# Feed-forward second projection: the last part as plain products by token blocks, sums on GpSimd, other places for the operands

## The chip, the cores and the metric

One Trainium2 chip, one core. The time is the device time of one execution in microseconds; of several executions the median is given. Matmuls run on TensorE (PE), the other work on VectorE (DVE), ScalarE (ACT) and GpSimd (POOL); SyncE (SP) issues transfers. Each of these engines takes its instructions in the order in which they stand in its own queue. Projections and their sums use PSUM banks of 128x512 float32; everything else lies in SBUF or in DRAM.

## What is computed

One encoder layer, windowed attention and a SwiGLU feed-forward network, on a sequence of 2048 tokens with D = 1024 and a hidden width of 2816, all in float32:

```
def swiglu(h, w_in, w_out):
    a, b = jnp.split(h @ w_in, 2, axis=-1)
    return (jax.nn.silu(a) * b) @ w_out

        x = x + g1 * rmsnorm(y, mix_norm_post[i])
        h = rmsnorm(x, ffn_norm_pre[i]) * (1.0 + sc2) + sh2
        y = swiglu(h, ffn_w_in[i], ffn_w_out[i])
        x = x + g2 * rmsnorm(y, ffn_norm_post[i])
```

The change concerns `swiglu` and the last line alone.

## The kernel before

A float32 operand is split into a part `hi`, rounded to fp32r, and the rest `lo` (`split`, L152 a cast on ACT, L153 a subtraction on DVE), and a product is three matmuls: hi·hi, hi·lo, lo·hi. On top of that both projections use Strassen-Winograd's scheme: of a 2x2 block product with operands a11, a12, a21, a22 (weights) and b11, b12, b21, b22 (activations), seven products of sums and differences are made where plain multiplication makes eight. For it the weights need s1 to s4, the activations t1 to t4, and the results seven sums.

**First projection.** The sequence is worked in two halves of 1024 tokens. A half has 22 hidden blocks `Hidden` (seven steps, pc0 to pc6, of 12 matmuls each, L147 to L149, into 6 PSUM banks); the last two blocks of a half are interleaved with the loading of the next half's operands (`interleaved`). ACT copies the first step's bank out (`take`, p1, L823); the other steps are added up by DVE. Two blocks make a pair of gated activations b11, b12, b21, b22, and `give_pair` stores its seven operands b11, t3, b22, t1, b21, t2, t4 in DRAM (g_d): for parts in `SPLIT` already split (a cast gh on ACT, a subtraction gl on DVE, two transfers, L799 and L800), else whole (one transfer). Between the stores the differences are formed in place on POOL and DVE.

**Second projection.** For each half the 11 pairs are taken in four parts of 2 or 3 pairs (`PARTS`, (hf, p) names a part, m its pairs). A part has seven stages, one for each product; a stage has four token blocks of 128, and a block m x 3 matmuls into one of 6 banks po (L1031 to L1033). In a half's first part ACT copies the banks to 28 result tiles z (L1036), later parts add to them on DVE (L1038). In a half's last part, as soon as the results of a block are complete, `SUMS` adds seven of them up (L1042), four on DVE and three on POOL per block. `Weights` loads raw weights wr (1 MB each, L976), forms s1, s3, s2, s4 on POOL (L979, L980, L998, L1000) and splits them into 14 buffers wo; `Grams` loads the stored activations into 15 buffers g (L1018, with a split on arrival, or L1020, both halves at once). Both run four stages ahead of the products. `finish(hf, b)` ends a token block: loads of x, squares and their sum on ACT (L1062), the root by Ln and Exp (L1067, L1068), eight small operations of DVE, transposes px of x on PE (L1079), then on DVE the scaled result (L1080) and the sum with x (L1081), and the store of out (L1082). The first half's endings are dealt out between the products of part (1,0); those of the second half follow the last products.

**What sets the order.** The program is recorded and a scheduler puts the instructions of each engine in order by the readiness of their operands and by the place where they are written; a stretch marked `high_priority(offset=...)` is taken as if it were written earlier. Tiles of one tag are reused in a ring, so a load or a split waits for the last reader of the tile it replaces.

## Time and profile before

| | us |
|---|---|
| median of 3 executions | 2247.26 (2245.46 to 2250.28) |
| the profiled execution's own time | 2245.18 |
| its span, first to last instruction | 2243.4 |
| PE busy | 2062.5 (92% of the span) |
| DVE busy | 1645.6 (73%) |
| POOL busy | 1154.7 (51%) |
| ACT busy | 1077.6 (48%) |
| mean granted TensorE clock | 0.959 |
| second projection, first matmul | 1752.0 |
| last matmul of the second projection | 2216.84 |

Busy time counts instructions that run, not what they wait for. A row of a timeline gives the start, the duration, the engine and line, the output and the inputs, the count of alike instructions in a run, and in brackets how long the engine had stood idle before it and what released it. A row of a stretch gives its length and then, for PE, weight loads, DVE, ACT and POOL, the busy time and the number of instructions. A group's row gives busy time, mean duration in ns, and the idle time in front with what ended it.

### The profile page before, as it was taken

What the parts mean: (1) busy time and instruction counts of PE and PEld (TensorE: products, weight loads), DVE (VectorE), ACT (ScalarE), POOL (GpSimd) and SP (SyncE); (2) the same over time, 40 slices, a digit from 0 to 9 for tenths busy, and PEclk for the clock granted to TensorE, in tenths of its full rate; (3) what the DMA queues carried; (4) which work ended last, traced back from release to release, by engine and by line L of the source; (5) the groups of instructions that cost most, each with busy time, mean ns of one, the idle gap of its engine ahead of it and who ended that gap; (6) DMA issues with size and microseconds to landing.
All of it is one profiled execution on the core that took longest, in us unless ns stands there. A gap on an engine that the chain in (4) does not pass through costs nothing.

```text
span 2243.4 us, 28903 instructions
## 1 busy us (share of the span) xinstructions
PE 2062.5 (92%) x9351; PEld 1674.8 (75%) x9351; DVE 1645.6 (73%) x2554; ACT 1077.6 (48%) x2135; POOL 1154.7 (51%) x1018
## 2 busy tenths in 40 slices
PE   5897999999988887999999879999999399999996
PEld 4785788878777665778887768888888288878885
DVE  7667665576768378876778898878785769695669
ACT  4536566686778545343434544444342554243222
POOL 3305444465986666866676655555552513353322
PEclk8997999999999998999999989999999699999998
DMA  7898867566564753545445854434342744659653
GB/s 260 238 273 286 260 162 219 148 204 183 174 200 149 220 174 122 177 138 171 163 158 185 285 187 162 148 137 165 129 170 76 264 145 154 241 207 366 247 204 131
DMA packets 287139, 431.01 MB, mean 192 GB/s; under 512 B 86739, under 2 KB 153868, under 8 KB 284940
## 3 DMA queue, kind: packets, MB, share of 16 engines
q1 hardware_dynamic: 286988, 429.16, 57.9%
q8 instruction: 74, 1.21, 0.2%
q14 instruction: 77, 0.63, 0.1%
HBM read 291.16 MB, written 137.92 MB: 191 GB/s over the span
## 4 chain that ended last, share of the span: by engine, by line
PE 32%; DVE 8%; POOL 4%; issue 4%; DMA 3%; ACT 2%; SPq 0%; POOLq 0%; DVEq 0%; ACTq 0%
PE pc_i L147 6%; PE pc_i L148 6%; PE pc_i L149 6%; PE po L1031 4%; PE po L1033 4%; PE po L1032 4%; DVE z L1042 1%; DMA wr<-w_out 1%; DVE z L1038 1%; DVE z L1080 1%; DVE wo_s L153 1%; DVE wo_a L153 1%; DMA ly<-y_d 1%; DVE wa_i L153 1%; POOL ws L979 0%
## 5 line engine op out<-in xcount | busy, mean ns | idle before, releaser
L147 PE MATMUL pc_i<-ht,ws_i 128*128 128x512 f32 x528 | 208.6, 396 | 6.7 <-ACT p_i L823 6.7
L148 PE MATMUL pc_i<-ht,ws_i 128*128 128x512 f32 x528 | 207.4, 393 | 0.9 <-DVE ht L153 0.9
L149 PE MATMUL pc_i<-ht,ws_i 128*128 128x512 f32 x528 | 207.4, 393 | 0.0
L456 DVE CUSTOM_DVE_ANT_0 pr<-s,bias,nsink 128x288 f32<-128x288 f32 (+3 forms) x256 | 123.5, 497 | 66.8 <-PE s L453 55.4
L458 ACT ACTIVATE pr<-pr,nm 128x289 f32<-128x289 f32 (+3 forms) x256 | 135.2, 530 | 74.0 <-DVE nm L456 65.2
L462 POOL TENSOR_SCALAR pr<-pr,rs 128x288 f32<-128x288 f32 (+3 forms) x256 | 138.7, 562 | 61.8 <-DVE rs L460 61.7
L153 DVE TENSOR_TENSOR wa_i<-wiri,wa_i 128x512 fp32r<-128x512 f32 x132 | 148.9, 1128 | 21.4 <-ACT wa_i L152 21.4
L1038 DVE TENSOR_TENSOR z<-po,z 128x512 f32<-128x512 f32 x168 | 113.5, 684 | 51.6 <-PE po L1033 50.1
L153 DVE TENSOR_TENSOR ws_i<-s_i,ws_i 128x512 fp32r<-128x512 f32 x132 | 136.6, 1035 | 19.4 <-ACT ws_i L152 19.2
L1031 PE MATMUL po<-wo_s,g 128*128 128x512 f32 x352 | 137.5, 394 | 11.6 <-ACT wo_s L152 11.0
L148 PE MATMUL pc_i<-hb,wa_i 128*128 128x512 f32 x352 | 139.1, 395 | 3.7 <-DVE hb L153 3.7
L1032 PE MATMUL po<-wo_s,g 128*128 128x512 f32 x352 | 138.2, 393 | 4.0 <-DVE wo_s L153 4.0
L149 PE MATMUL pc_i<-hb,wa_i 128*128 128x512 f32 x352 | 139.1, 395 | 1.8 <-DVE wa_i L153 1.8
L147 PE MATMUL pc_i<-hb,wa_i 128*128 128x512 f32 x352 | 139.7, 397 | 0.0
L1033 PE MATMUL po<-wo_s,g 128*128 128x512 f32 x352 | 138.0, 392 | 0.0
L475 PE MATMUL t<-ident,pr 128*128 128x128 f32 x736 | 118.6, 283 | 17.5 <-DVE plo L153 7.0
L979 POOL TENSOR_TENSOR ws<-wr 128x512 f32<-128x512 f32 x22 | 32.2, 1464 | 195.4 <-DMA wr<-w_out 195.4
L153 DVE TENSOR_TENSOR plo<-t,phi 128x512 fp32r<-128x512 f32 x184 | 121.9, 681 | 14.7 <-ACT phi L152 13.6
L152 ACT CAST wa_i<-wiri 128x512 fp32r<-128x512 f32 x132 | 81.5, 618 | 106.1 <-PE pc_i L149 103.1
L852 POOL TENSOR_TENSOR p_i<-p_i,u_i 128x512 f32<-128x512 f32 x44 | 67.0, 1523 | 126.0 <-issue 64.9
L453 PE MATMUL s<-k,q 128*128 128x288 f32 (+4 forms) x512 | 115.8, 326 | 15.7 <-DVE nm L456 15.3
L152 ACT CAST ws_i<-s_i 128x512 fp32r<-128x512 f32 x132 | 81.5, 618 | 93.6 <-PE pc_i L149 88.7
(281 smaller groups left out, 6391.4 us busy)
## 6 DMA issues: line engine op xcount, KB each, us to landing
wiri<-w_in SPq DMA_DIRECT2D x88, 512.0 KB, 4.6
g<-g_d_t SPq DMA_DIRECT2D x56, 512.0 KB, 5.4
ada<-ada_w SPq DMA_DIRECT2D x48, 512.0 KB, 5.7
wr<-w_out SPq DMA_DIRECT2D x22, 1024.0 KB, 8.9
g<-g_d_b SPq DMA_DIRECT2D x42, 512.0 KB, 4.9
q_d<-eq SPq DMA_DIRECT2D x64, 256.0 KB, 4.9
q<-q_d SPq DMA_DIRECT2D x16, 1024.0 KB, 6.8
wor<-w_o SPq DMA_DIRECT2D x32, 512.0 KB, 4.5
```

The costliest lines, as they stand in the source:

```text
L147: pe.matmul(ps, w[0], h[0], start=first, stop=False)
L148: pe.matmul(ps, w[0], h[1], start=False, stop=False)
L149: pe.matmul(ps, w[1], h[0], start=False, stop=last)
L152: act.copy(hi, src)
L153: return eng.tensor_tensor(lo, src, f(hi), ALU.subtract).ins
L456: dve.tensor_tensor_reduce(pr[:, i, lo:hi], ps[:, :n], bias[g][:, lo - starts[i]:hi - starts[i]], -1.0, nsink[:, g:g + 1], ALU.add, ALU.mi ...
L458: act.activation(pr[:, i, lo:hi + 1], pr[:, i, lo:hi + 1], AF.Exp, bias=nm[:, i:i + 1], scale=-1.0, accum_out=rs[:, i:i + 1])
L462: pool.tensor_scalar(pr[:, i, lo:hi], pr[:, i, lo:hi], rs[:, i:i + 1], 1.0, ALU.mult, ALU.mult)
L1031: pe.matmul(ps, g[:, 0], w[:, 0], start=k == 0, stop=False)
L1032: pe.matmul(ps, g[:, 0], w[:, 1], start=False, stop=False)
L1033: pe.matmul(ps, g[:, 1], w[:, 0], start=False, stop=k == m - 1)
L1038: dve.tensor_tensor(z[hf, b, name], ps, z[hf, b, name], ALU.add)
```

## The change

Five edits that belong together:

- The last part (1,3), pairs 9 and 10 of the second half, is no longer made by Strassen-Winograd but as plain products, `plain(j, b)`: eight times 24 matmuls, straight into the results' places. Its pairs are stored as b11, b12, b21, b22 without differences, and its weights are used as they are.
- The sums are all on POOL, seven for a block. The first half's stay in part (0,3); the second half's move from (1,3) to (1,2).
- `finish` takes one row block of 128 tokens (j, b) and multiplies by the gain row before the root is known; the second half's endings follow block by block behind `plain`.
- Part (0,3), pairs 8 to 10 of the first half, is stored whole and split when it is loaded.
- The pools rp (raw weights), gp (activations) and wo (weights) are opened on one side and in this order; wo has 11 buffers, gp 12, and three stages ahead are put at the start, the weights written ahead of the activations.

```diff
-SPLIT = ((0, 3), (1, 0), (1, 1), (1, 2), (1, 3))
+LAST = (1, 3)
+SPLIT = ((1, 0), (1, 1), (1, 2), (1, 3))
...
+        if (hf, part_of[hf][j][0]) == LAST:
+            for n in b:
+                give(n, b[n], False)
+            return
...
+    PLAIN = (("a11", "b11"), ("a12", "b21"), ("a21", "b12"), ("a22", "b22"))
-    SUMS = {"1": (("2", "1", pool),), "6": (("6", "1", dve), ("1", "6", "5", pool)),
-            "7": (("7", "6", dve), ("4", "7", pool), ("5", "7", dve)), "3": (("3", "1", dve),)}
+    SUMS = {"1": (("2", "1"),), "6": (("6", "1"), ("1", "6", "5")), "7": (("7", "6"), ("4", "7"), ("5", "7")),
+            "3": (("3", "1"),)}
-    WB, GB, G0 = 14, 15, 5
-
+    WB, GB = 11, 12
+
+    rp = open_pool(ctx, "rp")
+    gp = open_pool(ctx, "gp")
     wo = open_pool(ctx, "wo")
-    gp = open_pool(ctx, "gp")
-    rp = open_pool(ctx, "rp", side="right")
...
+                if (hf, p) == LAST:
+                    self.src.append(dict(a11=a11, a12=a12, a21=a21, a22=a22))
+                    continue
...
-        if p == len(PARTS[hf]) - 1:
-            for x, *y, eng in SUMS.get(name, ()):
+        if (hf, p) in ((0, len(PARTS[0]) - 1), (1, len(PARTS[1]) - 2)):
+            for x, *y in SUMS.get(name, ()):
                 y = [x] + y if len(y) == 1 else y
-                eng.tensor_tensor(z[hf, b, x], z[hf, b, y[0]], z[hf, b, y[1]], ALU.add)
+                pool.tensor_tensor(z[hf, b, x], z[hf, b, y[0]], z[hf, b, y[1]], ALU.add)
...
+    def plain(j, b):
+
+        hf, p = LAST
+        for i in range(2):
+            ps = psO.tile([P, CH], F32, tag="p", name=f"pl{j}_{b}_{i}")
+            m = PARTS[hf][p]
+            for k in range(m):
+                for e in range(2):
+                    g = [grams.g[hf, p, x, k] for x in range(4) if PLAIN[x][1] == f"b{e + 1}{j + 1}"][0][:, :, b * P:(b + 1) * P]
+                    w = [wts.w[hf, p, x, k] for x in range(4) if PLAIN[x][0] == f"a{i + 1}{e + 1}"][0]
+                    pe.matmul(ps, g[:, 0], w[:, 0], start=k == e == 0, stop=False)
+                    pe.matmul(ps, g[:, 0], w[:, 1], start=False, stop=False)
+                    pe.matmul(ps, g[:, 1], w[:, 0], start=False, stop=k == m - 1 and e == 1)
+            y = z[hf, b, PLACE[i, j]]
+            dve.tensor_tensor(y, ps, y, ALU.add)
+
+    def finish(hf, j, b):
+
+        c = hf * CPH + j
+        x1 = yp.tile([P, KT, P], F32, tag="x1", name=f"x1_{c}_{b}", bufs=3)
+        sp.dma_start(x1, x1_d[c][:, :, b * P:(b + 1) * P])
         yield
...
+        for i in range(2):
+            sq = yp.tile([P, CH], F32, tag="sq", name=f"sq{c}_{b}_{i}", bufs=2)
+            act.activation(sq, ys[i], AF.Square, scale=D ** -0.5, accum_out=ss[:, i:i + 1])
+            dve.tensor_tensor(ys[i], ys[i], grow[:, i * CH:(i + 1) * CH], ALU.mult)
+            px.append(psF.tile([P, CH], F32, tag="mm", name=f"px{c}_{b}_{i}"))
+            for k in range(JB):
+                pe.transpose(px[i][:, k * P:(k + 1) * P], x1[:, i * JB + k, :], ident)
+        dve.scalar_tensor_tensor(v, ss[:, :1], EPS, ss[:, 1:], ALU.add, ALU.add)
         act.activation(r, v, AF.Ln)
         act.activation(r, r, AF.Exp, scale=-0.5)
...
+        for i in range(2):
+            dve.scalar_tensor_tensor(ys[i], ys[i], r, px[i], ALU.mult, ALU.add)
+            (act if hf and i else sp).dma_start(out[c, b, :, i * CH:(i + 1) * CH], ys[i])
+        yield
...
     with tc.high_priority(offset=400):
-        grams.load(4)
-        wts.put(4)
+        wts.put(3)
+        grams.load(3)
...
+    last = [finish(LAST[0], j, b) for j in range(CPH) for b in range(JB)]
+    next(last[0])
+    for n, (j, b) in enumerate((j, b) for j in range(CPH) for b in range(JB)):
+        plain(j, b)
+        for f_ in last[n + 1:n + 2]:
+            next(f_)
+        for _ in last[n]:
+            pass
```

Line numbers behind the change differ: the casts and subtractions of `split` are L153 and L154, the copy p1 L828, the copies z L1048, the additions z L1050, the sums L1054, the weights' operations L991, L992, L1010 and L1012.

ACT, at the change of halves in the first projection: before (gh0_10 is the splitting of the first half's last pair for its store, hb and ht the next half's operands, ws, wa weights, p1_i1_0 the copy of the next half's first bank).

```order
L152 CAST ws2_i1_2_12907<-s2_i1_2_12898 128x512
L152 CAST gh0_10_t3_12526<-u2_i0_20_12267 128x512
L152 CAST gh0_10_b22_12531<-u2_i0_21_12282 128x512
L152 CAST wa12_i1_2_12910<-wiri1_2_12894 128x512
L152 CAST ws3_i1_2_12913<-wiri1_2_12894 128x512
L152 CAST gh0_10_t1_12538<-p1_i0_20_12221 128x512
L152 CAST gh0_10_b21_12543<-p1_i0_21_12236 128x512
L152 CAST ws1_i1_2_12916<-s1_i1_2_12897 128x512
L152 CAST gh0_10_t2_12550<-u2_i0_21_12282 128x512
L152 CAST wa22_i1_2_12919<-wiri1_2_12894 128x512
L152 CAST gh0_10_t4_12555<-p1_i0_21_12236 128x512
L823 COPY p1_i1_0_12620<-pc0_i1_0_12607 128x512
```

The same place on ACT after the change:

```order
L153 CAST ht41_3_12442<-ht41_3_12442 128x512
L153 CAST ws4_i1_0_12533<-s4_i1_0_12510 128x512
L153 CAST ws4_i1_1_12671<-s4_i1_1_12648 128x512
L853 ACTIVATE u2_i0_20_12227<-u2_i0_20_12227 128x512
L853 ACTIVATE u2_i0_21_12242<-u2_i0_21_12242 128x512
L153 CAST hb221_0_12489<-hb221_0_12489 128x512
L828 COPY p1_i1_0_12549<-pc0_i1_0_12536 128x512
L153 CAST wa11_i1_2_12833<-wiri1_2_12823 128x512
L153 CAST hb221_1_12493<-hb221_1_12493 128x512
L153 CAST hb221_2_12497<-hb221_2_12497 128x512
```

The casts gh0_10 are gone, and the copy p1_i1_0 stands directly behind the first of the last four operand casts.

ACT, at the start of the second projection, before: the first copies of results, z0_0_5 and on, and what stands ahead of them (wo0_1 and g0_1 are the weights and activations of the second part, (0,1)).

```order
L152 CAST g0_1_0_1_16392<-g0_1_0_1_16392 128x512
L152 CAST wo0_1_s1_0_16376<-ws0_1_0_16363 128x512
L152 CAST g0_1_0_2_16396<-g0_1_0_2_16396 128x512
L152 CAST wo0_1_s1_1_16380<-ws0_1_1_16368 128x512
L1050 COPY growt_16171<-pgrow_16169 8x128
L1036 COPY z0_0_5_16182<-po0_0_0_0_16175 128x512
L1036 COPY z0_1_5_16191<-po0_0_0_1_16184 128x512
L1036 COPY z0_2_5_16200<-po0_0_0_2_16193 128x512
L1036 COPY z0_3_5_16209<-po0_0_0_3_16202 128x512
L1036 COPY z0_0_2_16232<-po0_0_1_0_16225 128x512
```

The same place after the change (g0_0_4 to g0_0_6 are the activations of the first part's last stages):

```order
L153 CAST g0_0_4_1_16142<-g0_0_4_1_16142 128x512
L153 CAST g0_0_5_0_16188<-g0_0_5_0_16188 128x512
L153 CAST g0_0_5_1_16192<-g0_0_5_1_16192 128x512
L153 CAST g0_0_6_0_16238<-g0_0_6_0_16238 128x512
L153 CAST g0_0_6_1_16242<-g0_0_6_1_16242 128x512
L1062 COPY growt_16042<-pgrow_16040 8x128
L1048 COPY z0_0_5_16053<-po0_0_0_0_16046 128x512
L1048 COPY z0_1_5_16062<-po0_0_0_1_16055 128x512
L1048 COPY z0_2_5_16071<-po0_0_0_2_16064 128x512
L1048 COPY z0_3_5_16080<-po0_0_0_3_16073 128x512
L1048 COPY z0_0_2_16103<-po0_0_1_0_16096 128x512
```

The copies stood behind casts of part (0,1), weights included; now they stand behind casts of activations of part (0,0), and the weights of (0,1) come later.

POOL, at the end of the first half's sums, before (z0_b_n are results, ws1_0 and wr1_0 weights of part (1,0), ws1_1 and wr1_1 of part (1,1)):

```order
L980 TENSOR_TENSOR wr1_0_2_17745<-wr1_0_2_17745 128x512
L998 TENSOR_TENSOR ws1_0_2_17747<-ws1_0_2_17747,wr1_0_2_17745 128x512
L1042 TENSOR_TENSOR z0_0_4_16407<-z0_0_4_16407,z0_0_7_16467 128x512
L1000 TENSOR_TENSOR wr1_0_2_17745<-wr1_0_2_17745,ws1_0_2_17747 128x512
L1042 TENSOR_TENSOR z0_1_4_16416<-z0_1_4_16416,z0_1_7_16476 128x512
L1042 TENSOR_TENSOR z0_2_4_16425<-z0_2_4_16425,z0_2_7_16485 128x512
L1042 TENSOR_TENSOR z0_3_4_16434<-z0_3_4_16434,z0_3_7_16494 128x512
L979 TENSOR_TENSOR ws1_1_0_18427<-wr1_1_0_18425 128x512
L980 TENSOR_TENSOR wr1_1_0_18425<-wr1_1_0_18425 128x512
```

The same place after the change:

```order
L1054 TENSOR_TENSOR z0_1_4_16262<-z0_1_4_16262,z0_1_7_16337 128x512
L1054 TENSOR_TENSOR z0_1_5_16062<-z0_1_5_16062,z0_1_7_16337 128x512
L1054 TENSOR_TENSOR z0_0_3_16388<-z0_0_3_16388,z0_0_1_16153 128x512
L1054 TENSOR_TENSOR z0_1_3_16397<-z0_1_3_16397,z0_1_1_16162 128x512
L1054 TENSOR_TENSOR z0_2_4_16271<-z0_2_4_16271,z0_2_7_16346 128x512
L1054 TENSOR_TENSOR z0_2_5_16071<-z0_2_5_16071,z0_2_7_16346 128x512
L1054 TENSOR_TENSOR z0_2_3_16406<-z0_2_3_16406,z0_2_1_16171 128x512
L1012 TENSOR_TENSOR wr1_0_2_17716<-wr1_0_2_17716,ws1_0_2_17718 128x512
L1054 TENSOR_TENSOR z0_3_3_16415<-z0_3_3_16415,z0_3_1_16180 128x512
L1054 TENSOR_TENSOR z0_3_4_16280<-z0_3_4_16280,z0_3_7_16355 128x512
L1054 TENSOR_TENSOR z0_3_5_16080<-z0_3_5_16080,z0_3_7_16355 128x512
L991 TENSOR_TENSOR ws1_1_0_18398<-wr1_1_0_18396 128x512
```

Between the last weights of (1,0) and the first of (1,1) the queue now holds the sums into z0_b_3 and z0_b_5 too, which DVE made before.

More of the change, by code (lines that the diff above doesn't have):

```diff
@@ L93, in encoder_layer @@
     part_of = [[(p, k) for p, m in enumerate(PARTS[i]) for k in range(m)] for i in range(S // HALF)]
-    g_d = [[{n: dram.tile([P, 2 if (i, part_of[i][j][0]) in SPLIT else 1, CH], F32, name=f"g_d{i}_{j}_{n}") for n in OPERANDS}
+    g_d = [[{n: dram.tile([P, 2 if (i, part_of[i][j][0]) in SPLIT else 1, CH], F32, name=f"g_d{i}_{j}_{n}") for n in OPERANDS + ("b12",)}
             for j in range(HT // 2)] for i in range(S // HALF)]
@@ L962, in encoder_layer, with names @@
     parts = [(hf, p) for hf in range(S // HALF) for p in range(len(PARTS[hf]))]
-    stages = [(part, i) for part in parts for i in range(len(PRODUCTS))]
+    stages = [(part, i) for part in parts for i in range(len(PLAIN if part == LAST else PRODUCTS))]
+    def names(part, i):
+        return (PLAIN if part == LAST else PRODUCTS)[i][:2]
     class Weights:
@@ L990, in put @@
                     self.load(hf, p)
-                name = PRODUCTS[i][0]
+                name = names((hf, p), i)[0]
                 for k, src in enumerate(self.src):
@@ L998, in put @@
                         pool.tensor_tensor(src["s2"], src["s1"], src["a11"], ALU.subtract)
-                    elif name == "a12":
+                    elif name == "a12" and (hf, p) != LAST:
                         pool.tensor_tensor(src["s4"], src["a12"], src["s2"], ALU.subtract)
@@ L1004, in __init__ @@
         def __init__(self):
-            self.at, self.n, self.g = 0, G0, {}
+            self.at, self.n, self.g = 0, 0, {}
         def load(self, n=1):
@@ L1013, in load @@
                 for k in range(PARTS[hf][p]):
-                    d = g_d[hf][sum(PARTS[hf][:p]) + k][PRODUCTS[i][1]]
+                    d = g_d[hf][sum(PARTS[hf][:p]) + k][names((hf, p), i)[1]]
                     t = gp.tile([P, 2, CH], F32R, tag=f"g{self.n % GB}", name=f"g{hf}_{p}_{i}_{k}")
@@ L1048, in make_row @@
         pe.transpose(pg[:KT, :P], coef[:, 3, :], ident)
-        t = yp.tile([P, CH], F32, tag="sq", name="growt", bufs=1)[:KT, :P]
+        t = yp.tile([P, CH], F32, tag="sq", name="growt", bufs=2)[:KT, :P]
         act.copy(t, pg[:KT, :P])
@@ new lines, in finish @@
+    def finish(hf, j, b):
+        c = hf * CPH + j
+        x1 = yp.tile([P, KT, P], F32, tag="x1", name=f"x1_{c}_{b}", bufs=3)
+        sp.dma_start(x1, x1_d[c][:, :, b * P:(b + 1) * P])
+        yield
+        ss = yp.tile([P, 2], F32, tag="ss", name=f"ss{c}_{b}", bufs=3)
+        v, r, t = (yp.tile([P, 1], F32, tag=n, name=f"{n}{c}_{b}", bufs=3) for n in ("v", "r", "t"))
+        ys, px = [z[hf, b, PLACE[i, j]] for i in range(2)], []
+        for i in range(2):
[6 more added lines that the diff above has]
+        dve.scalar_tensor_tensor(v, ss[:, :1], EPS, ss[:, 1:], ALU.add, ALU.add)
@@ L1067, in finish @@
         act.activation(r, v, AF.Ln)
         act.activation(r, r, AF.Exp, scale=-0.5)
-        dve.tensor_tensor(t, r, r, ALU.mult)
-        dve.tensor_tensor(t, t, v, ALU.mult)
+        dve.scalar_tensor_tensor(t, r, v, r, ALU.mult, ALU.mult)
         dve.tensor_scalar(t, t, -0.5, 1.5, ALU.mult, ALU.add)
@@ L1073, in finish @@
         yield
-        for j in range(CPH):
-            for i in range(2):
-                y = z[hf, b, PLACE[i, j]]
-                px = psF.tile([P, CH], F32, tag="mm", name=f"px{hf}_{j}_{b}_{i}")
-                for k in range(JB):
-                    pe.transpose(px[:, k * P:(k + 1) * P], x1[j][:, i * JB + k, :], ident)
-                dve.scalar_tensor_tensor(y, y, r[:, j:j + 1], grow[:, i * CH:(i + 1) * CH], ALU.mult, ALU.mult)
-                dve.tensor_tensor(y, px, y, ALU.add)
-                sp.dma_start(out[hf * CPH + j, b, :, i * CH:(i + 1) * CH], y)
-            yield
+        for i in range(2):
+            dve.scalar_tensor_tensor(ys[i], ys[i], r, px[i], ALU.mult, ALU.add)
+            (act if hf and i else sp).dma_start(out[c, b, :, i * CH:(i + 1) * CH], ys[i])
+        yield
     tc.keep_in_program_order(act.preload_act_table_set("natural_log_exp_and_others"))
@@ L1098, in encoder_layer @@
             grams.load()
-        if p == len(PARTS[hf]) - 1:
-            end = chain(*(finish(hf, b) for b in range(JB)))
-    for b in range(JB):
-        for i in range(len(PRODUCTS)):
-            product(*parts[-1], i, b)
-            if b == 0:
-                wts.put()
-                grams.load()
-            next(end, None)
-        end = chain(end, finish(parts[-1][0], b))
-    for _ in end:
-        pass
+        if (hf, p) == (0, len(PARTS[0]) - 1):
+            end = chain(*(finish(hf, j, b) for b in range(JB) for j in range(CPH)))
+    wts.put()
+    grams.load()
+    last = [finish(LAST[0], j, b) for j in range(CPH) for b in range(JB)]
[6 more added lines that the diff above has]
+            pass
 def _bucket(n):
```

11 lines of the change are left out of this document (removed).

## The prediction

> **What bounds the kernel now.** I read the stretches of the span first (busy time of each engine, instruction counts in brackets, then granted TensorE clock, DMA share, GB/s), because the kernel is 92% TensorE (PE) and the question is where that engine does not run.
>
> ```profile
> 1000.00:1150.00 150.00, 150.00 (x652) 122.23 (x651) 105.08 (x128) 58.39 (x95) 103.61 (x73) 1.00 0.49 162
> 1150.00:1250.00 100.00, 96.82 (x412) 78.06 (x411) 78.37 (x89) 42.30 (x70) 70.60 (x48) 0.98 0.55 190
> 1250.00:1350.00 100.00, 80.40 (x327) 64.08 (x327) 89.90 (x110) 47.64 (x85) 55.79 (x35) 0.90 0.63 223
> 1740.00:1790.00 50.00, 15.62 (x45) 10.46 (x44) 40.55 (x42) 26.10 (x48) 29.91 (x20) 0.67 0.75 271
> 1820.00:1877.00 57.00, 57.00 (x253) 47.20 (x252) 47.60 (x64) 25.54 (x44) 18.37 (x12) 1.00 0.45 148
> 1934.00:1991.00 57.00, 57.00 (x253) 47.21 (x252) 43.50 (x51) 13.02 (x24) 33.78 (x22) 1.00 0.69 249
> 1991.00:2053.00 62.00, 57.78 (x271) 47.12 (x270) 48.88 (x89) 31.81 (x78) 19.82 (x14) 0.97 0.82 297
> 2217.00:2243.40 26.40, 8.94 (x41) 6.65 (x40) 21.44 (x41) 3.48 (x12) 4.25 (x3) 0.64 0.53 179
> ```
>
> The undisturbed first projection issues 652 matmuls in 150 us, 0.230 us each; a part of the second projection 253 in 57 us, 0.225 us each. By that measure PE loses time in three places. The change of halves: 100 us hold 435 slots, 412 and 327 were used, so 23 and 108 are lost, **30 us** together. The passage between the projections: 50 us hold 222, 45 were used, **40 us** lost. The end: 26 us without a projection matmul. The parts between are full, apart from 4 us at 1991 to 2053. So only these places can give much, and any new stall elsewhere is a loss outright.
>
> Who ends the waits (start, duration, engine, line; in brackets idle time before and its releaser), PE first, then the engines followed back:
>
> ```profile
> 1274.53 0.79 PE L147 MATMUL pc_i<-ht,ws_i 128*128 128x512 f32 x1 [6.71 <-ACT p_i L823]
> 1317.53 0.51 PE L148 MATMUL pc_i<-ht,wa_i 128*128 128x512 f32 x1 [2.47 <-DVE ht L153]
> 1328.69 0.80 PE L147 MATMUL pc_i<-hb,ws_i 128*128 128x512 f32 x1 [10.42 <-ACT p_i L823]
> ...
> 1327.53 0.62 ACT L152 CAST gh_t<-p_i 128x512 fp32r<-128x512 f32 x1 [2.35 <-issue]
> 1328.06 0.58 ACT L823 COPY p_i<-pc_i 128x512 f32<-128x512 f32 x1
> ```
>
> At the change of halves PE waits for ScalarE (ACT) to empty a PSUM bank (p_i, L823), and that copy stands in ACT's queue behind casts gh_t, the splitting of the first half's last pair for its store. At 1328 the copy starts as the cast ends.
>
> ```profile
> 1752.00 2.07 PE L1031 MATMUL po<-wo_s,g 128*128 128x512 f32 x4 [10.99 <-ACT wo_s L152]
> 1788.15 0.79 PE L1031 MATMUL po<-wo_a,g 128*128 128x512 f32 x1 [17.93 <-ACT z L1036]
> ...
> 1782.01 0.62 ACT L152 CAST wo_s<-ws 128x512 fp32r<-128x512 f32 x1 [8.27 <-POOL ws L979]
> ...
> 1786.85 0.62 ACT L152 CAST wo_s<-ws 128x512 fp32r<-128x512 f32 x1 [3.69 <-POOL ws L979]
> ...
> 1780.72 1.26 POOL L979 TENSOR_TENSOR ws<-wr 128x512 f32<-128x512 f32 x1 [7.25 <-DMA wr<-w_out]
> ```
>
> In the passage PE first waits 10.99 us for the first weights, then 17.93 us for z copies (L1036). These stand on ACT behind casts of the *next* part's weights, which wait for GpSimd (POOL) and it for the raw weights' DMA.
>
> **The change part by part.** The sum is made against the profiled execution: span 2243.4, its own time 2245.18, the median of the runs shown 2247.26, so a median reads 2 us above it.
>
> *Change of halves.* Pairs 8 to 10 of the first half are no longer split when stored: 21 casts leave ACT and 21 subtractions VectorE (DVE). In the new order of ACT the copies p1 of blocks 20, 21 and of the next half's first block stand behind no gh cast. This takes the waits of 6.71 and 10.42 us, and the lower clock behind them (granted 0.90 in that stretch). What remains is operand loading, shown by the wait of 2.47 us on ht, and the stores before in-place subtractions, which the earlier pairs do without a stall. I leave 10 us of the 30: **−20 us**. Bounds: −6 if the DVE queue is late next wherever ACT was, −27 if only the 2.47 us and its like remain.
>
> *Passage.* The weights of stages 0 to 2 are now put ahead of the operands in the program, and their pool lies where the order lets them be split before the last matmul pc; the waits of 10.99 and 17.93 lose their cause. Next is late what the first product needs from DRAM, g of stage 0, written by a store of the last pairs and read back, cast and subtracted:
>
> ```profile
> g<-g_d_t SPq DMA_DIRECT2D x32, 256.0 KB, 3.4
> ...
> L153 DVE TENSOR_TENSOR g<-g 128x512 fp32r<-128x512 f32 x56 | 49.0, 895 | 7.8 <-ACT g L152 7.6
> L152 ACT CAST g<-g 128x512 fp32r<-128x512 f32 x56 | 33.9, 619 | 17.9 <-DMA g<-g_d_t 10.4 <-DMA g<-g_d_b 6.8
> ```
>
> A load of 3.4 us, two casts of 0.62, two subtractions of 0.90: 6.4 us, with one us of queueing some 7. A second wait stays: on ACT the first z copy stands behind the casts of stage 6 (g0_0_6), whose buffer (12 now, two for a stage) comes free when stage 0 is done. 24 matmuls (5.4 us), a load and two casts later, 10 us after the first product, the copies begin; PE has six banks and stops after 36 matmuls, 8.1 us, so some 3 to 6 us are lost. I take 13 us instead of 40: **−27 us**, with bounds −15 (that second wait as long as today's 17.93) and −33 (7 us alone).
>
> *Sums on POOL, first half.*
>
> ```profile
> L1042 POOL TENSOR_TENSOR z<-z,z 128x512 f32<-128x512 f32 x24 | 33.1, 1378 | 92.6 <-DVE z L1038 68.2 <-DVE z L1042 17.4 <-DVE t L1069 3.8
> L1042 DVE TENSOR_TENSOR z<-z,z 128x512 f32<-128x512 f32 x32 | 31.0, 984 | 0.2
> L1038 DVE TENSOR_TENSOR z<-po,z 128x512 f32<-128x512 f32 x168 | 113.5, 684 | 51.6 <-PE po L1033 50.1
> ...
> 1953.47 1.29 POOL L1042 TENSOR_TENSOR z<-z,z 128x512 f32<-128x512 f32 x1 [33.27 <-DVE z L1038]
> ...
> 1968.56 1.74 POOL L980 TENSOR_TENSOR wr<-wr 128x512 f32<-128x512 f32 x1
> ...
> 1995.57 1.28 POOL L1042 TENSOR_TENSOR z<-z,z 128x512 f32<-128x512 f32 x1 [2.44 <-DVE z L1042]
> ...
> 1998.69 0.63 ACT L1062 ACTIVATE sq<-z 128x512 f32<-128x512 f32 x1 [9.77 <-DVE z L1042]
> ```
>
> Sixteen sums leave DVE (16 × 0.98 = 16 us) and POOL takes them (16 × 1.38 = 22 us). POOL is busy 34 of the 57 us of part (0,3), so it becomes full: its queue from 1953 holds 28 sums and 12 operations on weights, 40 by some 1.55 us (the rows have 1.29 to 1.74) = 62 us, to about 2015 where 1997 was. The squares (L1062) wait for these sums, and the z copies of part (1,0) stand between the squares on ACT; with six banks (8.2 us) of cover, 18 us of lateness leave about 10 us of stall where 4 are now: **+6 us**. DVE there loses 16 and gets 21 subtractions for the part now loaded whole, 21 × 0.90 = 19 us: 43.5 becomes 47 of 57, still hidden. The bounds are 0 (the squares come late but copies are interleaved) and +18 (all the lateness shows).
> The Trainium skill, page "GPSIMD Engine Reference", section "4.1 Engine selection", speaks against this part: an elementwise operation with two inputs belongs on VectorE, GpSimd being about twice as slow. The rows here have 1378 against 984 ns, 1.4 times; by the page's two the 28 sums would take 55 us instead of 39, an estimate, and the term would be about +22.
>
> *Last part.* The plain form has 192 matmuls for 168 (24 × 0.225 = +5.4 us). The ending by blocks is spread through the part:
>
> ```profile
> 2216.84 0.39 PE L1033 MATMUL po<-wo_s,g 128*128 128x512 f32 x1
> ...
> 2166.00:2217.30 51.30, 3.10 (x24) 2.79 (x24) 1.00 0.31 103
> 2217.30:2243.40 26.10, 8.72 (x40) 6.65 (x40) 0.64 0.54 181
> ...
> L1080 DVE SCALAR_TENSOR_TENSOR z<-z,r,grow 128x512 f32<-128x512 f32 x32 | 21.9, 748 | 0.2
> L1062 ACT ACTIVATE sq<-z 128x512 f32<-128x512 f32 x32 | 20.2, 631 | 52.6 <-POOL z L1042 41.5 <-DVE z L1042 10.3 <-DVE t L1071 0.6
> ...
> 2004.02 0.19 ACT L1067 ACTIVATE r<-v 128x2 f32<-128x2 f32 x1
> ...
> 2232.42 0.15 DVE L1069 TENSOR_TENSOR t<-r 128x2 f32<-128x2 f32 x1
> ...
> 2239.48 0.69 DVE L1081 TENSOR_TENSOR z<-px,z 128x512 f32<-128x512 f32 x1 [0.16 <-PE px L1079]
> ```
>
> (The two stretches count the transposes L1079 alone.) Today 24 of the second half's 64 transposes come before the last product, at 3.10/24 = 0.129 us; 40 behind it. With one block's eight left for the end, 32 move forward: 32 × 0.129 = +4.1 us. Behind the last matmul then stand one addition (0.68), a square (0.63), v, two activations of 0.19 each, three small operations of 0.15, two scalar_tensor_tensor (1.5) and the 3.2 us that today lie between the end of the last DVE operation (2240.17) and the end of the span: with hand-over between engines 9 us instead of 26.2. A block's turn costs DVE two additions, two products with grow, two final ones and small ones, 2 × 0.68 + 2 × 0.68 + 2 × 0.75 + 0.8 = 5.0 us, less than PE's 24 × 0.225 + 8 × 0.129 = 6.4, so DVE hides. The second half's sums now run on POOL in part (1,2) and just behind it, 28 × 1.38 = 39 us, beside matmuls, and that part's weight sums vanish from POOL. Together +9.5 − 17.2 = **−8 us**; bounds −12 and 0 (a late fourth stage of weights, since eight operands of each kind must be there at once).
>
> *Shorter look-ahead* (three stages for four, 11 and 12 buffers for 14 and 15) brings raw weights one stage later, 36 × 0.225 = 8.1 us. The third piece of part (1,1) shows the least slack:
>
> ```profile
> 2041.99 1.28 POOL L979 TENSOR_TENSOR ws<-wr 128x512 f32<-128x512 f32 x1
> ...
> L979 POOL TENSOR_TENSOR ws<-wr 128x512 f32<-128x512 f32 x22 | 32.2, 1464 | 195.4 <-DMA wr<-w_out 195.4
> ```
>
> That is 11 us before that part begins (2053); 8 us later, plus cast and subtraction of 1.6, it is just in time. I cost it at nothing, hidden by those 11 us; without them it is up to 8 us for each of six boundaries.
>
> Sum: −20 − 27 + 6 − 8 = −49. 2245.2 − 49 = 2196, on the median's footing **2198 us**.
>
> **The rivals.**
> A. *The stall at the change of halves keeps its length*, because DVE or the operand loads are late wherever ACT was: DVE is busy 89.9 of the 100 us there, which speaks for it; that the waits name ACT, and the copy starts at a cast's end, speaks against. Gain there 6 instead of 20: 2212.
> B. *POOL becomes the bound*: all of its lateness shows, at the first half's end 18 and at the start of the last part 10 more. For: POOL is full there, 34 + 22 of 57 us. Against: later weights arrive by DMA only after POOL's queue ends. 2198 + 12 + 10 = 2220.
> C. *The passage only changes its wait*: z copies behind casts stay late by today's 17.93, gain 15: 2210.
> D. *Slower*: the look-ahead is the price. If the raw weights' slack is under one stage at all six boundaries, each costs 8.1 us, 49 in all, which cancels the sum; with A or C beside it 2247 + 14 = 2261. It decides from a slack below 8 us. For: 11 us is near it, and POOL is fuller. Against: a PE that stalls gives the weights time back, and POOL at L979 waits 195.4 us over 22 pieces for that DMA today without a wait of PE in the middle parts.
> E. *It does not do what it says*: if the new order put the old splits elsewhere in ACT's queue, only the tail's 8 would be left: 2239.
>
> **How the numbers follow.** Forecast 0.52 (2185 to 2208), A 0.13, C 0.12, B 0.11, D 0.07, E 0.05. All but D, and a part of E, end below. About 0.2%, 4.5 us, is what a measurement of this kernel can tell from no change; the chances are faster 0.89, same 0.05, slower 0.06. The range reaches from 2176 (the better bounds of passage and halves together, −13, and some of the tail's) to 2228, within B.
>
> **What would show it.** Right: in the profile after, the stretch 1250 to 1350 has over 380 matmuls; no wait of PE over 8 us in the passage; copies of z wait behind g casts there; the sums on POOL run in one queue of about 60 us at the first half's end; under 10 us lie behind the last matmul. Wrong: long waits of PE named POOL z or wr in the parts, PE below 55 of 57 us in a middle part, or the wait of 10 us at the change of halves still there under another releaser.

## The result and the profile after

The changed kernel takes 2195.77 us (median of 4 executions, 2194.22 to 2197.30) against 2247.98 before (4 executions, 2245.46 to 2250.28): ratio 0.9768, 95% interval 0.9751 to 0.9785. The prediction was 2198 us, 2176 to 2228. The profiled executions have spans of 2195.5 and 2243.4 us.

To see where the 47.9 us of span went, marks are set in the two PE timelines by counting matmuls: the 1512th and the 2016th of the first projection's 3696 (18 and 24 hidden blocks of 84; the change of halves lies between), its last one, and the last one of each part. The stretches between them:

| stretch, us | before | after | difference | forecast |
|---|---|---|---|---|
| start to 18 blocks (not touched by the change) | 1207.1 | 1212.8 | +5.7 | 0 |
| 18 to 24 blocks, with the change of halves | 146.0 | 124.0 | −22.1 | −20 |
| 24 blocks to the end of the first projection | 387.9 | 388.2 | +0.2 | 0 |
| passage: from there to the end of part (0,0) | 79.1 | 51.7 | −27.3 | −27 |
| parts (0,1) to (0,3) | 171.4 | 171.4 | 0.0 | 0 |
| part (1,0) | 70.8 | 75.3 | +4.5 | +6 |
| parts (1,1) and (1,2) | 114.2 | 114.2 | 0.0 | 0 |
| part (1,3) | 40.8 | 49.9 | +9.1 | +9.5 |
| behind the last product | 26.2 | 8.0 | −18.1 | −17.2 |

The first row varies from kernel to kernel, though nothing in it differs: 1207.1 to 1214.5 us over the fourteen profiles of this study. So single stretches tell more here than medians that differ by less than some 5 us.

Stretches of after (busy time and instruction counts of PE, weight loads, DVE, ACT, POOL; granted clock, DMA share, GB/s). By the marks, part (0,1) begins at 1777, part (0,3) runs from 1891 to 1948 and part (1,0) begins there:

```profile
1250.00:1350.00 100.00, 96.60 (x403) 76.94 (x402) 89.25 (x108) 46.34 (x84) 66.03 (x42) 0.97 0.61 212
...
1722.00:1772.00 50.00, 41.56 (x162) 32.93 (x161) 36.67 (x42) 33.65 (x64) 20.45 (x14) 0.90 0.73 244
1777.00:1834.00 57.00, 57.00 (x253) 47.23 (x252) 49.00 (x66) 25.75 (x44) 18.67 (x12) 1.00 0.44 149
1891.00:1948.00 57.00, 57.00 (x253) 47.23 (x252) 46.51 (x63) 20.70 (x35) 34.36 (x23) 1.00 0.56 194
1948.00:2010.00 62.00, 54.26 (x255) 45.14 (x254) 51.46 (x83) 30.61 (x82) 37.94 (x26) 0.94 0.73 256
...
1916.00:1973.00 57.00, 54.36 (x243) 45.04 (x242) 46.87 (x50) 19.02 (x46) 55.09 (x37) 0.97 0.69 240
...
2149.00:2187.50 38.50, 38.50 (x196) 32.33 (x195) 28.57 (x63) 11.27 (x38) 0.00 (x0) 1.00 0.43 140
2187.50:2195.50 8.00, 0.84 (x8) 0.60 (x6) 3.41 (x9) 1.13 (x4) 0.00 (x0) 0.87 0.32 119
```

The hole at the change of halves holds 403 matmuls where 327 were, the passage 162 where 45 were. POOL is busy 34 of the 57 us of part (0,3), as before, and 55 of the 57 us from 1916 to 1973: the sums begin 20 us into that part and run on into part (1,0). PE's waits in these places, from the timeline of after:

```profile
1309.72 0.50 PE L149 MATMUL pc_i<-hb,ws_i 128*128 128x512 f32 x1 [0.93 <-DVE hb L154]
1313.08 0.79 PE L149 MATMUL pc_i<-hb,ws_i 128*128 128x512 f32 x1 [2.40 <-DVE hb L154]
...
1727.32 0.51 PE L1043 MATMUL po<-wo_s,g 128*128 128x512 f32 x1 [2.39 <-DVE wo_s L154]
1730.21 0.80 PE L1043 MATMUL po<-wo_s,g 128*128 128x512 f32 x1 [2.16 <-DVE u_i L847]
1744.81 0.50 PE L1043 MATMUL po<-wo_a,g 128*128 128x512 f32 x1 [3.89 <-ACT z L1048]
...
1961.75 1.97 PE L1097 MATMUL px<-ident,x 128*128 128x128 f32 x8 [2.64 <-DVE z L1106]
1978.89 1.97 PE L1097 MATMUL px<-ident,x 128*128 128x128 f32 x8 [5.10 <-DVE z L1106]
...
2187.08 0.39 PE L1078 MATMUL pl<-wo_a,g 128*128 128x512 f32 x1
2187.31 1.03 PE L1097 MATMUL px<-ident,x 128*128 128x128 f32 x8
```

The waits of 6.71 and 10.42, of 10.99 and of 17.93 us are gone; what is late next are the operands hb, then in the passage three waits of 2 to 4 us, and in part (1,0) the transposes px, whose two banks wait for the last operation of an ending.

### The profile page after: what moved, and what is told of

Read it like the earlier page. It is cut to its first block, busy times and chain, and to the rows that moved or that the text cites. A ratio compares the mean times of both kernels' runs of the same rounds, so it can differ in the third digit from the quotient of the medians.

```text
span 2195.5 us, 28863 instructions
## 1 busy us (share of the span) xinstructions
PE 2058.7 (94%) x9375; PEld 1675.1 (76%) x9375; DVE 1610.0 (73%) x2510; ACT 1073.3 (49%) x2139; POOL 1185.4 (54%) x1038
## 3 DMA queue, kind: packets, MB, share of 16 engines
q1 hardware_dynamic: 280220, 409.76, 56.9%
## 4 chain that ended last, share of the span: by engine, by line
PE 65%; DVE 11%; DMA 8%; POOL 6%; issue 5%; ACT 3%; SPq 1%; DVEq 0%; POOLq 0%; ACTq 0%
PE pc_i L149 9%; PE pc_i L148 9%; PE pc_i L150 9%; PE po L1043 5%; PE po L1044 5%; PE po L1045 5%; PE psq L148 2%; PE psq L149 2%; PE psq L150 2%; PE t L476 2%; PE s L454 2%; PE py L150 2%; PE py L149 2%; PE py L148 2%; PE o L481 1%
## 5 line engine op out<-in xcount | busy, mean ns | idle before, releaser
L154 DVE TENSOR_TENSOR ws_i<-s_i,ws_i 128x512 fp32r<-128x512 f32 x132 | 136.6, 1035 | 31.4 <-ACT ws_i L153 31.2
L154 DVE TENSOR_TENSOR wa_i<-wiri,wa_i 128x512 fp32r<-128x512 f32 x132 | 146.9, 1113 | 14.8 <-ACT wa_i L153 14.8
L154 DVE TENSOR_TENSOR plo<-t,phi 128x512 fp32r<-128x512 f32 x184 | 122.0, 682 | 13.9 <-ACT phi L153 12.8
L153 ACT CAST wa_i<-wiri 128x512 fp32r<-128x512 f32 x132 | 81.6, 619 | 101.7 <-PE pc_i L150 99.1
L1043 PE MATMUL po<-wo_s,g 128*128 128x512 f32 x320 | 126.5, 395 | 4.6 <-DVE wo_s L154 2.4
L1044 PE MATMUL po<-wo_s,g 128*128 128x512 f32 x320 | 125.7, 393 | 0.0
L1045 PE MATMUL po<-wo_s,g 128*128 128x512 f32 x320 | 124.5, 392 | 0.0
L1050 DVE TENSOR_TENSOR z<-po,z 128x512 f32<-128x512 f32 x140 | 94.6, 685 | 35.0 <-PE po L1045 33.4
L454 PEld LDWEIGHTS s<-k,q 128*128 128x128 f32 x512 | 88.4, 202 | 41.6 <-DVE nm L457 30.9
L153 ACT CAST ws_i<-s_i 128x512 fp32r<-128x512 f32 x132 | 81.3, 618 | 77.5 <-PE pc_i L150 75.1
```

The lines of the kernel that those rows point to most:

```text
L153: act.copy(hi, src)
L154: return eng.tensor_tensor(lo, src, f(hi), ALU.subtract).ins
L454: m = pe.matmul(ps[:, :n], qs, kk[:, e, jb * P + lo:jb * P + hi], start=e == 0, stop=e == 1)
L1043: pe.matmul(ps, g[:, 0], w[:, 0], start=k == 0, stop=False)
L1044: pe.matmul(ps, g[:, 0], w[:, 1], start=False, stop=False)
L1045: pe.matmul(ps, g[:, 1], w[:, 0], start=False, stop=k == m - 1)
```

## The experiments

All times are medians with the kernel before run beside them; stretches are read as in the table above. In each diff `+` and `-` are against the kernel that the sentence names.

**Part (0,3) split again**, the changed kernel otherwise:

```diff
-SPLIT = ((1, 0), (1, 1), (1, 2), (1, 3))
+SPLIT = ((0, 3), (1, 0), (1, 1), (1, 2), (1, 3))
```

> The changed kernel with one edit undone: pairs 8 to 10 of the first half are split again before they are stored (part (0,3) back in SPLIT). If the split casts in ACT's queue were the cause of the stall at the change of halves, the waits of PE for the copy p1 come back, the last matmul of the first projection ends about 16 us later, and the median is 2212 (2207 to 2216); part (0,3) keeps its 57.1 us, since its loads were hidden. Rival: the gain there came from the other places of the pools or from the order as a whole, and the median stays within 3 us of 2196.

2219.70 us (2218.1 to 2222.9); ratio 0.9879, 0.9862 to 0.9897. From 18 to 24 blocks 146.8 us (before 146.0, after 124.0): the edit is the whole gain there, 22.9 us, more than the 16 expected, and the median lies above the expected range. Part (0,3) keeps its 57.1.

**The same edit alone, on the kernel before** (`(0, 3)` taken out of its SPLIT):

> The kernel before with one edit alone: part (0,3) stored whole. If that edit is worth what the change of halves lost, the last matmul of the first projection ends 16 us earlier, the passage stays at 79 us, part (0,3) at 57 us, and the median is 2231 (2227 to 2235). Rival: without the other edits VectorE has the 16 sums of the first half and the 21 subtractions of the loads in part (0,3) together, 43.5 + 19 = 62 of 57 us, and 5 us or more come back: 2236 to 2240.

2225.39 us (2222.7 to 2228.5); ratio 0.9903, 0.9885 to 0.9922. The change of halves takes 125.5 us, the passage 74.0, part (0,3) 57.1. The edit brings 20.5 us by itself and 5 more in the passage, so the median lies below the expected range; VectorE's 62 us of work do not show, so the rival falls.

**Split again, with the casts on GpSimd.** Which part of the splitting holds PE? Against the run with (0,3) split again:

```diff
-            split(hi, lo, t, dve)
+            if hf == 0:
+                pool.tensor_copy(hi, t)
+                dve.tensor_tensor(lo, t, f(hi), ALU.subtract)
+            else:
+                split(hi, lo, t, dve)
```

> The changed kernel with part (0,3) stored split again, but with the casts of the first half's split pairs made on GpSimd instead of ACT; the subtractions on VectorE and the doubled transfers are back as before. If the casts in ACT's queue alone made the stall at the change of halves, the waits for the copy p1 stay short there and the median is 2196 to 2203. If what holds PE is the rest of the splitting (VectorE's subtractions and the last pair's chain, in which the buffers and the operands of the next half wait), the waits of 8 and 10 us come back under one releaser or another and the median is 2212 to 2222, as with the casts on ACT (2219.7).

2226.22 us (2225.6 to 2229.5), above both expected ranges, and 157.4 us from 18 to 24 blocks: no gain, 10.5 us worse than with the casts on ACT. In its timeline the copies of p1 stand behind no cast of the splitting, and ACT idles in front of them (rows of ACT, then of PE, then a cast of the splitting on POOL):

```profile
1285.72 0.59 ACT L832 COPY p_i<-pc_i 128x512 f32<-128x512 f32 x1 [1.40 <-DMA g_d_b<-gl_b]
1287.13 0.59 ACT L832 COPY p_i<-pc_i 128x512 f32<-128x512 f32 x1 [0.82 <-DMA g_d_t<-p_i]
...
1339.30 0.59 ACT L832 COPY p_i<-pc_i 128x512 f32<-128x512 f32 x1 [10.87 <-DVE gl_b L801]
...
1286.36 0.80 PE L148 MATMUL pc_i<-ht,ws_i 128*128 128x512 f32 x1 [16.23 <-ACT p_i L832]
1339.94 0.79 PE L148 MATMUL pc_i<-hb,ws_i 128*128 128x512 f32 x1 [12.55 <-ACT p_i L832]
...
1333.37 1.01 POOL L800 CAST gh_t<-u_i 128x512 fp32r<-128x512 f32 x1 [1.82 <-DVE u_i L813]
```

A copy that reads a PSUM bank waits here for work on a split operand because of its output tile. p1 comes from the ring `temp` of 10 tiles, and a split pair takes 7 tiles gh and 3 tiles gl from the same ring, each free only when its store has landed and its subtraction has read it; a pair stored whole takes none. So the splitting can hold the copy in two ways: by casts ahead of it on ACT, and by the ring. The run shows that the second holds it when the first is gone. It doesn't show what held it in the kernel before, because the splitting itself is late here: the last pair's first cast of a difference stands at 1333.37 us, and at 1318.11 in the kernel before.

What held the copy in the kernel before can be read there. Here are the first of the two waits (a cast of the splitting, and the copy, with three other casts between), then for the second the difference that its last cast reads and the store that frees the copy's output tile; that cast and that copy are the rows at 1327.53 and 1328.06 shown ahead of the result:

```profile
1271.82 0.62 ACT L152 CAST gh_t<-p_i 128x512 fp32r<-128x512 f32 x1 [2.24 <-DVE p_i L810]
...
1273.90 0.57 ACT L823 COPY p_i<-pc_i 128x512 f32<-128x512 f32 x1
...
1325.71 1.74 DVE L810 TENSOR_TENSOR p_i<-p_i,u_i 128x512 f32<-128x512 f32 x1
...
1319.90 0.32 SPq L800 DMA_DIRECT2D g_d_t<-u_i  x1
```

VectorE's difference ends at 1327.45 us, the cast of its result starts at 1327.53 and the copy at 1328.06, 0.53 us behind, which is the distance of casts that wait for nothing (1319.15, 1319.67, 1320.19). The store had landed at 1322.20 us by the updates of its semaphore, 5.9 us earlier. So it is the cast ahead on ACT, waiting for VectorE, that held the copy. With (0,3) split again in the changed kernel it is the same: cast at 1332.87, copy at 1333.40, tile free at 1327.54. At the first wait the tile was free at 1268.50, 5.4 us ahead of the copy.

**First half's sums mixed again** (the changed kernel, with the old four sums on DVE and three on POOL per block, for hf == 0 only):

> The changed kernel with the first half's sums again four on VectorE and three on GpSimd per block; the second half's stay on GpSimd. If the sums on GpSimd cost the 4.5 us by which part (1,0) is longer, the part falls from 75.3 to about 71 us and the median to 2191. Rival 1: the stall there belongs to the order of the endings (two PSUM banks px, which wait for the last operation of the block before), not to GpSimd: part (1,0) stays at 75 and the median at 2196. Rival 2: VectorE, with 16 us of sums and 19 us of operand subtractions in part (0,3), becomes late: (0,3) is longer than 57.1 us and the median is 2198 to 2203.

2191.82 us (2190.9 to 2194.5); ratio 0.9755, 0.9739 to 0.9772. Part (1,0) falls from 75.3 to 71.1 us, part (0,3) stays at 57.1: the sums on GpSimd cost 4.2 us, and VectorE hides both its burdens. This is the fastest kernel of the study; its interval overlaps that of the changed kernel, so the 4.2 us of the stretch are the surer number.

**Old places, order and look-ahead** (the changed kernel with the five lines of WB, GB, the pools and the start as before, and one buffer for sq so that it fits):

> The changed kernel with the old places: wo and gp on the left, rp on the right, 14 and 15 buffers, four stages ahead with the activations written first, and one buffer for sq instead of two so that it fits. If the places and the order bring the 27 us of the passage between the projections, the stretch from the last matmul of the first projection to the end of part (0,0) grows from 52 to 75 us or more and the median is 2218 (2213 to 2224). Rival: the 27 us come from the last pairs' plain storing, which takes casts, subtractions and transfers out of the queues just there; then the stretch stays under 57 us and the median is 2196 to 2201.

2201.55 us (2199.8 to 2204.7); ratio 0.9800, 0.9779 to 0.9821. The passage takes 57.0 us, not 75, at the edge of the rival's 57, and the median lies just above the rival's range. In PE's timeline the first wait is back, the second isn't:

```profile
1733.29 2.07 PE L1043 MATMUL po<-wo_s,g 128*128 128x512 f32 x4 [10.27 <-ACT wo_s L153]
...
1748.17 0.50 PE L1043 MATMUL po<-wo_a,g 128*128 128x512 f32 x1 [2.60 <-ACT z L1048]
```

This spoke against the prediction's reason for the passage, and I formed theory W: the last pairs' storing work makes the waits. Five runs on it follow.

**The last part's edits alone** (everything else as in the kernel before, but one buffer for sq):

> The kernel before with the last part's edits alone: plain products, endings by blocks, the second half's sums on GpSimd in part (1,2); part (0,3) split, the first half's sums mixed, old places and order (one buffer for sq). Expected from the parts measured so far: the change of halves as before, the passage 57 to 62 us by theory W (79 by theory P), part (1,0) 71, the last part and what lies behind it 9 us shorter; median 2219 (2214 to 2224) by W, 2239 by P.

2219.30 us (2217.1 to 2220.7); ratio 0.9868, 0.9850 to 0.9885. The passage takes 56.9 us, part (1,0) 70.1, the last part 49.8 and 8.1 behind it, as W has it.

**The old storing work put back**, into the changed kernel and into the one with old places:

```diff
-            for n in b:
-                give(n, b[n], False)
+            b11, b12, b21, b22 = (b[n] for n in ("b11", "b12", "b21", "b22"))
+            give("b11", b11, True)
+            give("b12", b12, True)
+            pool.tensor_tensor(b11, b12, b11, ALU.subtract)
+            dve.tensor_tensor(b12, b22, b12, ALU.subtract)
+            give("t3", b12, False)
+            give("b22", b22, True)
...
+            give("t2", b22, False)
```

> The changed kernel, in which the last two pairs get their old work back at the end of the first projection: per pair four differences and seven operands split and stored (b11, b12, b22, b21 and three differences; the differences are stored and not used, the split of the four is made again on loading... the last part therefore reads what the split store left in its places). Places, order and look-ahead stay new. Theory W, after the run with the old places: the waits of the passage come from that work, which stands in the queues of ACT, VectorE and SyncE ahead of the second projection's loads: the passage (last matmul of the first projection to the end of part (0,0)) grows from 52 to 62 us or more, median 2206 to 2216. Theory P, as predicted before: the places and the order shield the passage; it stays under 56 us, median 2196 to 2201.

> The same work put back into the kernel with the old places, order and look-ahead. Theory W: the passage goes from 57 us (old places alone) to 72 us or more, close to the 79 of the kernel before, median 2217 to 2226. If it stays under 62 us, the difference to the kernel before lies in neither places nor this work, but in another edit (the endings' buffers, the order that the scheduler makes of the whole).

New places: 2206.50 us (2202.8 to 2208.8), passage 58.9, neither theory's bound. Old places: 2211.81 us (2211.4 to 2213.3), passage 65.8, again between. The work costs 7 to 9 us. Up to the kernel before with part (0,3) stored whole (74.0 us), as it is here too, 8 us are missing. The wait for a copy z in the second one, from PE's timeline, and on ACT the first cast of ws, behind the copies:

```profile
1757.23 0.80 PE L1053 MATMUL po<-wo_a,g 128*128 128x512 f32 x1 [4.80 <-ACT z L1058]
...
1767.16 1.14 ACT L153 CAST wo_s<-ws 128x512 fp32r<-128x512 f32 x2 [6.38 <-POOL ws L1001]
```

**The chain's last link too**, t4 split and stored, in the kernel with the old places:

```diff
             give("t2", b22, False)
+            give("t4", b21, False)
```

> The kernel with the old places and the old storing work, as in the run before, and with the last difference t4 split and stored too, the end of the chain. In its order the cast of the next part's first weights stands ahead of the first copies of results on ACT again, as in the kernel before. If that order is the rest of the 79 us, the passage is 73 to 80 us, PE waits 12 us or more for a copy z, and the median is 2220 to 2228; if only the amount of work counts, one more operand of 7 adds 1 to 2 us to the 65.8, median 2213.

2219.00 us (2216.6 to 2220.5; its profile has a span of 2214.8), passage 73.9; the median is 1 us under the expected range. PE's two long waits in it, and on ACT the cast directly ahead of the first copies z:

```profile
1735.91 2.08 PE L1054 MATMUL po<-wo_s,g 128*128 128x512 f32 x4 [13.16 <-ACT wo_s L153]
...
1764.83 0.79 PE L1054 MATMUL po<-wo_a,g 128*128 128x512 f32 x1 [15.09 <-ACT z L1059]
...
1763.53 0.62 ACT L153 CAST wo_s<-ws 128x512 fp32r<-128x512 f32 x1 [10.20 <-POOL ws L1002]
```

One operand more, and the wait for a copy z goes from 4.80 to 15.09 us. With it the cast wo0_1_s1_0, of the next part's first weights, stands ahead of the first copy z on ACT; without it, behind. The cast waits 10.20 us for GpSimd, and the copies wait with it: the order makes the wait, as in the kernel before, not the amount of work. The 73.9 us are the 74.0 of the kernel before with (0,3) stored whole, so no difference to it remains.

**The new places alone, on the kernel before** (rings of 11 and 12, three stages, weights first; the last part's loop turned stage by stage, its endings behind all products):

> The kernel before with the new places, rings of 11 and 12, three stages ahead and weights first, and nothing else new but the loop of the last part, which is turned stage by stage (with block by block it needs 14 buffers of each kind at once); its endings come after all products. What is read is the passage. Theory W, from the runs so far: the places alone are worth the first wait, about 5 us net, since the last pairs' old storing still holds the loads and the copies: passage 68 to 76 us. Theory P, as predicted: the waits of 10.99 and 17.93 us lose their cause with the places and the order: passage 52 to 58 us. Whatever the passage, the turned loop adds some 10 us or more behind the last matmul.

2228.59 us (2223.3 to 2230.1); ratio 0.9897, 0.9881 to 0.9913. The turned loop costs behind the last product (41.8 us for 26.2), as expected. But the passage takes **46.2 us**, the shortest of all and below theory P's 52, with all the old storing work in it and a single wait of PE:

```profile
1750.97 0.77 PE L1031 MATMUL po<-wo_s,g 128*128 128x512 f32 x1 [5.37 <-DVE u_i L842]
```

Theory W's claim for this run falls, P's stands: places and order by themselves remove both waits. That the storing work makes them with the old places (57.0 us without it, 73.9 with it) stands too. The 5.5 us less than in the changed kernel go with ACT's order: here the copies z stand between casts of g and PE has no wait for them.

**Fourteen buffers for activations**, with the mixed sums; first simply `GB = 14`, then with the two extra buffers in a pool of their own behind the weights:

> The changed kernel with the first half's sums mixed again and 14 buffers for activations instead of 12, so that the casts of stage 6 (g0_0_6), ahead of the first copies of results on ACT, need no buffer of stage 0. If these casts caused the 3.9 us for which PE waits for the copies z, that wait goes and the passage falls from 51.5 to about 47 us: median 2187 to 2189, against 2191.8 for the mixed sums alone. If another operation takes its place in ACT's queue, 2191 to 2193.

> The changed kernel with the first half's sums mixed and 14 buffers for activations, the two more in a pool of their own behind the weights, so that the weights stay where the changed kernel has them. The first weights' wait of 13.4 us, which 14 buffers in front of them brought, should go (first product within 3 us of the last matmul of the first projection), and the copies z stand ahead of the casts of stage 6: passage 47 to 49 us, median 2186 to 2189, against 2191.8. If the copies still end behind another cast, passage 51 and median 2191 to 2193.

The first: 2196.53 us (2193.8 to 2198.0), passage 54.1. The wait for z is gone, but the first weights are late again, since two buffers more in front of wo move it over tiles that come free later. The second: 2196.39 us (2192.6 to 2197.4), passage 51.2: the weights are in time, and the copies z wait behind another cast, of the next part's activations (it reads t1 from g_d_t, where stage 6 reads b22). PE's wait in the first kernel:

```profile
1738.04 2.07 PE L1043 MATMUL po<-wo_s,g 128*128 128x512 f32 x4 [13.35 <-ACT wo_s L153]
```

PE's wait in the second, and the cast on ACT that the copies stand behind:

```profile
1746.88 0.50 PE L1044 MATMUL po<-wo_a,g 128*128 128x512 f32 x1 [3.56 <-ACT z L1049]
...
1744.82 1.38 ACT L153 CAST g<-g 128x512 fp32r<-128x512 f32 x2 [1.16 <-DMA g<-g_d_t]
```

Both are misses: neither beats the mixed sums alone.

## Why the prediction was right, and where its reasons were not

- **Change of halves** (−20 forecast, −22.1 measured). The size is right and the edit is the right one: alone it brings 20.5 us, taken back it costs 22.9. The reason is borne out too: in the kernel before the copy stands behind a cast gh_t, which waits for a difference of the same pair, and the copy's own tile was free 5.9 us earlier. What the prediction didn't see is that the splitting also fills the ring from which the copy takes its tile. With the casts moved to GpSimd that ring holds the copy, so clearing ACT's queue in this way brings nothing; storing the pair whole clears both. A larger ring wasn't tried.
- **Passage** (−27 forecast, −27.3 measured). That places and order remove both waits is shown by the run with them alone (46.2 us). What the prediction didn't see: the last part's edits, with their plain storing, do nearly the same without them (56.9), so the gains don't add: 33 us, 22 us and 5 us (part (0,3) stored whole) by themselves, 27 together. The remaining 13 us were mis-sized little in sum: the loss is 14 (51.7 less 168 matmuls at 0.225 = 38). But its parts differ. The 7 us ahead of the first product are 2.39 us, and 2.16 us behind it for a bank of the first projection. The wait for copies z is 3.9 us where 3 to 6 stood, behind the casts of stage 6 as forecast. That is 8.4 us; the rest is the lower granted clock behind these waits, which the sum left out. The rows of after's stretches, then of its ACT:

```profile
1725.00:1735.00 10.00, 5.52 (x13) 4.10 (x14) 9.99 (x12) 5.43 (x11) 4.94 (x3) 0.71 0.87 291
...
1745.00:1755.00 10.00, 10.00 (x38) 8.04 (x38) 1.92 (x2) 5.53 (x11) 3.87 (x3) 0.83 0.90 267
...
1742.97 1.15 ACT L153 CAST g<-g 128x512 fp32r<-128x512 f32 x2 [1.91 <-DMA g<-g_d_b]
...
1744.19 3.44 ACT L1048 COPY z<-po 128x512 f32<-128x512 f32 x7
```

- **Sums on POOL** (+6 forecast, +4.5 measured; 4.2 by the run with mixed sums). The length of the queue was read rightly: it runs from 1910.5 to 1975.3 us, 65 us where 62 stood. A sum takes 1506 ns in the mean of both halves, between the 1378 of the forecast and twice VectorE's 984. That POOL becomes full in part (0,3) was not right: it is busy 34 us there, as before, and full only behind its middle. The sums end 27 us behind part (0,3) (1975.3 against 1948.0) where they ended 5 us behind it, 22 us later, against 18 forecast. Most of that does not show in PE's time; the copies of part (1,0) lie between the squares (rows of POOL and ACT of after):

```profile
L1054 POOL TENSOR_TENSOR z<-z,z 128x512 f32<-128x512 f32 x56 | 83.0, 1506 | 57.7 <-DVE z L1050 57.4
...
1953.23 15.23 POOL L1054 TENSOR_TENSOR z<-z,z 128x512 f32<-128x512 f32 x10
...
1970.12 5.18 POOL L1054 TENSOR_TENSOR z<-z,z 128x512 f32<-128x512 f32 x3
...
1954.99 0.64 ACT L1093 ACTIVATE sq<-z 128x512 f32<-128x512 f32 x1 [6.32 <-POOL z L1054]
1955.62 0.57 ACT L1048 COPY z<-po 128x512 f32<-128x512 f32 x1
```

  Where it shows, it is not in the copies, as the term had it, but in the transposes px, whose banks wait for an ending that waits for POOL.
- **Last part** (+9.5 and −17.2 forecast, +9.1 and −18.1 measured). Both come with this part's edits alone (49.8 and 8.1 us there), and VectorE hides as forecast: it is busy 28.57 of the 38.5 us quoted.
- **Shorter look-ahead** (0 forecast). Every middle part takes 57.1 us in all fourteen profiles; of rival D nothing is seen. The slack had been read too small: by the marks part (1,1) begins at 2062.2 us in the kernel before, not at 2053, so its third piece of weights was 20 us ahead, not 11. In after it is 11.8 us ahead (2011.57 against 2023.4), one stage of 8 us less, as forecast:

```profile
2011.57 1.28 POOL L991 TENSOR_TENSOR ws<-wr 128x512 f32<-128x512 f32 x1 [1.65 <-DMA wr<-w_out]
```

- **The sum.** The stretches that the change touches add up to −53.7 us, where −49 was forecast, and the untouched start, late in the profile of after and early in that of before, gives 5.7 us back. That this pair of profiles comes so close to the sum is chance; the medians differ by 52.2 us. The low end of the range doesn't follow from the bounds that it names: −13 and the tail's −4 give 2181, and 2176 needs the sums' bound of 0 as well.

Rival A's rule (another thing is late where ACT was) shows in the run with the casts on GpSimd, where the ring took ACT's place; the edit itself escapes it, since a pair stored whole takes no tile of the ring. Rival B named what the sums do, at 18 and 10 us; they cost 4.5 at the one place and nothing at the other.

## What to carry to other kernels

A wait that names the engine which empties a bank can have two causes: what stands ahead of the copy on that engine, and what the copy's *output* tile waits for. Look up when each of them ended; the later one holds the copy, and when it is removed the other may be next. So count, too, how many tiles of its ring the work beside it takes. A chain of queues between two stages can be broken at several links, so the gains of two edits that break it aren't to be added, and undoing one of them understates it; try each alone on the kernel before as well. The size of a ring can be set by one loop far from where it hurts: the last part, block by block, needed 14 buffers of each kind, its plain form needs 8, and with 11 and 12 the weights lie where memory comes free early (with 14 buffers for activations in front of them they were 13.35 us late).
